# One more pair of every feed-forward way out by the seven-product scheme, the last pair's operands kept on chip, loads in a fixed order; FFN 2's pairs in another order with two more early products

## The chip, the cores and the metric

The kernel runs on one core of a Trainium2 chip. Its engines work side by side, each through its own instructions in order: TensorE (PE in the profile) multiplies, VectorE (DVE), ScalarE (ACT) and GpSimd (POOL) work on tiles, and SyncE (SP) issues nearly all transfers. An engine waits on semaphores that other engines or transfers raise. The metric is the device time of one execution in microseconds (us), lower is better. A difference below 0.2% (about 4 us) can't be told from no change here.

## The reference, cut to what matters

One layer on x of 1024 tokens by 1024 channels, in float32; D_FF is 2816:

```
x = x + 0.5 * swiglu_ffn(rms_norm(x, norm_ffn1), ffn1_w_in, ffn1_w_out)
x = x + token_mixer(rms_norm(x, norm_mix), w_in, w_out, ...)
x = x + 0.5 * swiglu_ffn(rms_norm(x, norm_ffn2), ffn2_w_in, ffn2_w_out)
return rms_norm(x, norm_final)

swiglu_ffn(x, w_in, w_out): gate, up = split(x @ w_in); return (silu(gate) * up) @ w_out
```

The change touches only the two feed-forward networks (FFN 1, FFN 2) and the last norm; the four token mixers between them stay.

## The kernel before, in words

**Precision.** Every operand of a product is split into a high and a low part in a reduced float32 (tiles `whi`/`wlo` for weights; the two halves of an `xs`, `xe` or `hx` tile for activations). ScalarE casts the high part, VectorE subtracts to get the low one, and `acc3` makes one product of three matmuls: weight-high with both parts, weight-low with the high one.

**Seven products.** The 2816 hidden channels are 22 tiles of 128, taken as 11 pairs p = 0 to 10. A two-by-two block product is done by seven products instead of eight (Strassen's scheme in Winograd's form), in the order ORDER7 = 1, 2, 5, 7, 6, 3, 4. `left` makes the weight sums (`wsum`) and operands for it; `seven` runs the products and adds results (ScalarE copies some out of PSUM, GpSimd adds the kept ones, VectorE adds the rest). In the way in, `pair` does gate and up of one pair so, 168 matmuls in all. For a few pairs products 1 and 2 (the corner) were done early, by `corner`: the first four (CORNERS) in the mixers and the next MORE at the start of FFN 2, before pair 0. Such a pair has 120 matmuls left.

**The way out.** The hidden values of a pair that goes out by seven products are added to seven combinations, split, and written to memory as seven tiles `hs` (`put_seven`, 512 KB each). `out_seven` reads them back: the nine pairs below STRASSEN = 9 go in blocks, first pair 0 alone, then four blocks of two pairs. A block has four quarters q of 256 output channels. A quarter loads its weights (`wraw`, 512 KB), makes operands, does seven products, and adds them onto the accumulators x (tiles `gr` and `gg`): ScalarE halves a product into a `tmp` or `hx` tile, VectorE adds onto x, GpSimd adds the rest (`plus`). The hidden values of pairs 9 and 10 are written plainly, loaded again, and multiplied by the ordinary way (96 matmuls a pair instead of 84) after the blocks. In FFN 2 `token_major` transposes x on TensorE ahead of that plain part, which works token tile by token tile: the first 512 output channels (c = 0) for eight token tiles tt, then the others (c = 1). Once a token tile has both, `final_sum` and `final_norm` make the last norm of it: GpSimd makes the factor `frs` in three small operations, VectorE scales both halves, SP and ScalarE send them out.

**Order.** The code is written in program order, and a scheduler then orders each engine's instructions by what is ready; where the code says `keep_in_program_order`, the order in the code stands. A tile name has a fixed number of buffers (bufs): a load into it waits until the buffer's last reader is done. SP takes its transfers in order, so what stands behind a waiting load waits as well.

Of the kernel before, what the change touches and what calls it, by code (L numbers as in the profile page):

```python
# [26 lines left out]
CORNERS, MORE, STRASSEN, URGENT = 4, 2, 9, 80  # L27
# [73 lines left out]
class Trunk:  # L101
# [26 lines left out]
    def wload(self, src, nk, c, splits=2):  # L128

        nc = self.nc  # L130
        raw = self.wp.tile([P, 1088], F32, name="wraw")
        rv = raw[:, :nk * c].rearrange("p (k c) -> p k c", c=c)
        for ap, off, n in src:
            nc.sync.dma_start(rv[:, :, off:off + (n or c)], ap)
        step = nk // splits
        res = []
        for s in range(splits):
            hi = self.wp.tile([P, 544], F32R, name="whi", bufs=4)
            lo = self.wp.tile([P, 544], F32R, name="wlo", bufs=4)
            sl = slice(s * step * c, (s + 1) * step * c)  # L140
            n = step * c
            nc.scalar.copy(hi[:, :n], raw[:, sl])  # L142
            nc.vector.tensor_tensor(lo[:, :n], raw[:, sl], hi[:, :n].bitcast(F32), op=ALU.subtract)  # L143
            for j in range(step):
                res.append((hi[:, j * c:(j + 1) * c], lo[:, j * c:(j + 1) * c]))
        return res
# [138 lines left out]
    def left(self, wk, raw, corner=False):  # L285
# [5 lines left out]
        def add(x, y, op):  # L291
            t = wk.tile([P, H], F32, name="wsum", bufs=3)
            nc.vector.tensor_tensor(t, x, y, op=op)
            return t

        def halves(a):
            hi = self.wp.tile([P, 544], F32R, name="whi", bufs=4)
            lo = self.wp.tile([P, 544], F32R, name="wlo", bufs=4)
            nc.scalar.copy(hi[:, :H], a)  # L299
            nc.vector.tensor_tensor(lo[:, :H], a, hi[:, :H].bitcast(F32), op=ALU.subtract)  # L300
            return [(hi[:, j * P:(j + 1) * P], lo[:, j * P:(j + 1) * P]) for j in range(4)]

        if not corner:
            yield halves(a11)
            yield halves(a12)
        s1 = add(a21, a22, ALU.add)
        yield halves(s1)
        s2 = add(s1, a11, ALU.subtract)
        yield halves(add(a11, a21, ALU.subtract))
        yield halves(s2)  # L310
        yield halves(add(a12, s2, ALU.subtract))
        yield halves(a22)
# [40 lines left out]
    def pair(self, wk, raws, right, p, p1=(None, None)):  # L353
# [9 lines left out]

        def up(i, h, ps, other):
# [3 lines left out]
            if p >= STRASSEN:  # L368
                self.put_h(u, 2 * p + i, h)

        def ups():
            if p1[0] is not None and p < STRASSEN:
# [3 lines left out]
            if p < STRASSEN:  # L376
                self.put_seven(wk, us, p)
# [3 lines left out]
    def put_seven(self, wk, us, p):  # L381
# [3 lines left out]
        def put(n, t):  # L385
            x = wk.tile([P, 2 * H], F32R, name="hx", bufs=3)
# [34 lines left out]
    def ffn1_in(self, wk, w_in):  # L421

        nc = self.nc
        self.xd, self.hd, self.hs, self.which = {}, {}, {}, 1
# [35 lines left out]
        for p in range(1, FT // 2):  # L460
            raws = [self.pair_weights(wk, w_in, p, o) for o in (0, DFF)]
            for t in self.pair(wk, raws, right, p):
# [17 lines left out]
    def ffn2_in(self, wk, w_in):  # L480

        nc = self.nc
        self.which, self.spare, self.turn, self.hs = 2, None, 0, {}
# [36 lines left out]
        for p in range(1, FT // 2):  # L520
            raws = [self.pair_weights(wk, w_in, p, o) for o in (0, DFF)]
            for t in self.pair(wk, raws, right, p, self.p1.get(p, (None, None))):
                for _ in t:
                    pass
# [27 lines left out]
    def out_seven(self, wk, w_out, slot, tmp):  # L552
# [4 lines left out]
        blocks = [(0, STRASSEN % 2)] if STRASSEN % 2 else []  # L557
        blocks += [(b, 2) for b in range(STRASSEN % 2, STRASSEN, 2)]

        def weights(b0, nb, q):  # L560

            raw = self.wp.tile([P, 1088], F32, name="wraw")[:, :nb * 512]
# [1208 lines left out]
```

## Time and profile before

| | us |
|---|---|
| three timed runs | 2102.67, 2103.93, 2104.75 (median 2103.93) |
| the profiled execution | 2101.29, of which 2099.5 is the span that the profile shows |
| TensorE busy | 1998.7 (95% of the span) |
| VectorE busy | 1491.5 (71%) |
| ScalarE busy | 966.2 (46%) |
| GpSimd busy | 417.3 (20%) |

TensorE works nearly all the time, so the time is made of its matmuls and of the stretches in which it waits. By the timeline FFN 1's way in runs to about 482 us and its way out to about 665 us, the mixers to about 1441 us, FFN 2's way in to about 1854 us and its way out to the end. In a row of the timeline the first number is the start, the second how long the group ran, and the brackets at its end tell how long the engine had been idle before it, and what it waited for.

### The profile page before, as it was taken

The page shows a single profiled execution, that of the slowest core. Times are in us where ns is not written, and L with a number is a line of the kernel's source. Part 1 is how long each engine was busy: PE and PEld are TensorE (multiplying, and loading weights), DVE is VectorE, ACT ScalarE, POOL GpSimd, SP SyncE. Part 2 cuts the span into 40 slices and gives each one's busy share as a digit, 9 for nine tenths or more (in the row PEclk, how much of TensorE's full clock was granted, in tenths as well). Part 3 has the DMA queues.
Part 4 walks back from the last instruction along what each step waited for, and adds up shares of the span by engine and source line. Part 5 has one row for each costly group of instructions (what it writes and reads, how often), then busy time and mean ns, then how long its engine had stood idle before and what let it go on. Part 6 is the DMA issues. An engine that isn't in the chain of part 4 may idle for free. (4 is left out here: it accounts for less than half of the span.)

```text
span 2099.5 us, 29339 instructions
## 1 busy us (share of the span) xinstructions
PE 1998.7 (95%) x10448; PEld 1603.6 (76%) x10448; DVE 1491.5 (71%) x2564; ACT 966.2 (46%) x1808; POOL 417.3 (20%) x430
## 2 busy tenths in 40 slices
PE   6999999998999999989999999899899999979998
PEld 4688888886887778777788787687677788868876
DVE  6967768656769556587665676667988877558784
ACT  6544444434434464443554534434544545334443
POOL 0100000004446502011020010100232200044461
PEclk9999999998999999999999999999999999989999
DMA  5444444448573453333452335544466545396632
GB/s 197 136 139 151 161 131 160 151 150 311 194 272 116 148 151 101 106 95 101 145 153 82 111 113 165 185 153 152 150 215 205 202 139 181 115 349 248 227 104 80
DMA packets 289139, 338.13 MB, mean 161 GB/s; under 512 B 27744, under 2 KB 216512, under 8 KB 288992
## 3 DMA queue, kind: packets, MB, share of 16 engines
q1 hardware_dynamic: 285888, 328.65, 47.2%
q0 software_dynamic: 1664, 4.95, 0.7%
q10 hardware_dynamic: 1440, 2.65, 0.3%
q8 instruction: 82, 1.34, 0.3%
q14 instruction: 65, 0.53, 0.1%
HBM read 225.83 MB, written 110.36 MB: 160 GB/s over the span
## 5 line engine op out<-in xcount | busy, mean ns | idle before, releaser
L86 PE MATMUL mm<-xs,whi 128*128 128x512 f32 x1664 | 546.4, 409 | 24.6 <-ACT whi L573 21.3
L86 PEld LDWEIGHTS mm<-xs,whi 128*128 128x128 f32 x1664 | 303.8, 191 | 97.5 <-ACT whi L573 23.0
L86 PE MATMUL mm<-xs,wlo 128*128 128x512 f32 x832 | 331.6, 399 | 2.8 <-DVE wlo L574 1.8
L86 PEld LDWEIGHTS mm<-xs,wlo 128*128 128x128 f32 x832 | 158.7, 191 | 43.1 <-DVE wlo L574 3.9
L86 PE MATMUL pq<-xs,whi 128*128 128x512 f32 x576 | 181.8, 397 | 3.6 <-ACT whi L299 3.6
L299 ACT CAST whi<-wsum 128x512 fp32r<-128x512 f32 x176 | 108.3, 620 | 160.4 <-PE pq L86 53.6
L142 ACT CAST whi<-wraw 128x512 fp32r<-128x512 f32 (+1 forms) x176 | 108.2, 620 | 155.2 <-PE mm L86 121.9
L143 DVE TENSOR_TENSOR wlo<-wraw,whi 128x512 fp32r<-128x512 f32 (+1 forms) x176 | 124.5, 714 | 64.9 <-ACT whi L142 41.6
L86 PE MATMUL px<-xs,whi 128*128 128x512 f32 x512 | 161.1, 396 | 0.0
L86 PE MATMUL pg<-xs,whi 128*128 128x512 f32 x496 | 157.5, 397 | 3.0 <-ACT xs L174 2.7
L300 DVE TENSOR_TENSOR wlo<-wsum,whi 128x512 fp32r<-128x512 f32 x176 | 119.3, 688 | 21.0 <-ACT whi L299 20.8
L86 PE MATMUL pq<-xe,whi 128*128 128x512 f32 x416 | 131.6, 398 | 0.8 <-DVE xe L175 0.8
L86 PEld LDWEIGHTS pq<-xs,whi 128*128 128x128 f32 x576 | 108.9, 190 | 29.7 <-ACT whi L299 5.2
L86 PE MATMUL pq<-xs,wlo 128*128 128x512 f32 x288 | 115.0, 399 | 5.7 <-DVE wlo L300 5.7
L339 POOL TENSOR_TENSOR tmp<-tmp 128x512 f32<-128x512 f32 x22 | 35.1, 1595 | 398.8 <-ACT tmp L329 398.8
L86 PEld LDWEIGHTS px<-xs,whi 128*128 128x128 f32 x512 | 96.9, 190 | 21.8 <-ACT whi L299 0.2
L86 PEld LDWEIGHTS pg<-xs,whi 128*128 128x128 f32 x496 | 93.9, 190 | 25.2 <-ACT xs L174 3.5
L300 DVE TENSOR_TENSOR wlo<-wraw,whi 128x512 fp32r<-128x512 f32 x64 | 44.0, 691 | 83.2 <-ACT whi L299 83.2
L339 POOL TENSOR_TENSOR gr<-gr 128x512 f32<-128x512 f32 x20 | 42.7, 2135 | 300.9 <-ACT gr L329 282.7
L86 PE MATMUL px<-xs,wlo 128*128 128x512 f32 x256 | 101.3, 396 | 0.1
L86 PE MATMUL pg<-xs,wlo 128*128 128x512 f32 x248 | 98.5, 397 | 0.0
L86 PE MATMUL px<-xe,whi 128*128 128x512 f32 x304 | 95.3, 394 | 0.3 <-ACT gr L329 0.3
(454 smaller groups left out, 4285.0 us busy)
## 6 DMA issues: line engine op xcount, KB each, us to landing
hs<-hx SPq DMA_DIRECT2D x126, 512.0 KB, 3.4
xs<-hs SPq DMA_DIRECT2D x94, 512.0 KB, 7.2
wraw<-in_ffn_w_in SPq DMA_DIRECT2D x56, 512.0 KB, 3.9
wraw<-in_w_in SPq DMA_DIRECT2D x52, 512.0 KB, 4.1
wrawb<-in_ffn_w_in SPq DMA_DIRECT2D x44, 512.0 KB, 4.6
wraw<-in_ffn_w_out SPq DMA_DIRECT2D x40, 512.0 KB, 3.6
xe<-hs SPq DMA_DIRECT2D x32, 512.0 KB, 7.1
wraw<-in_w_out SPq DMA_DIRECT2D x16, 512.0 KB, 4.1
```

Source lines behind the costliest of these rows:

```text
L86: return self._add(self.nc.tensor.matmul(out, lhsT=lhsT, rhs=rhs, **kw), n * 0.42e-3 if rhs.dtype == F32R else max(n * 1.68e-3, 0.04))
L142: nc.scalar.copy(hi[:, :n], raw[:, sl])
L143: nc.vector.tensor_tensor(lo[:, :n], raw[:, sl], hi[:, :n].bitcast(F32), op=ALU.subtract)
L299: nc.scalar.copy(hi[:, :H], a)
L300: nc.vector.tensor_tensor(lo[:, :H], a, hi[:, :H].bitcast(F32), op=ALU.subtract)
L339: nc.gpsimd.tensor_tensor(kept[5], kept[5], kept[7], op=ALU.add)
```

## The change

- Both ways out send ten pairs by seven products in five blocks of two, and one pair the plain way (`PLAIN`).
- FFN 1: the plain pair is p = 10. Its operands are split where they are made and stay in four `xs` tiles (`keep`), and it goes out first. Its weights, the x tiles and the first block's `hs` tiles are loaded in a fixed order. Then come the blocks (0,1), (2,3), (4,5), (6,7), (8,9). While a block runs, the next one's `hs` tiles are fetched in a fixed order too: two in each of the quarters 0 to 2, and the other eight in quarter 3 (`early` = 6).
- FFN 2: the plain pair is p = 0 and goes out last. The way in goes through the pairs in the order 0, 1, 8, 2, 3, 9, 4, 5, 6, 7, 10. The seven tiles of pair 10 stay on chip, those of pair 9 are loaded back during pair 10, and the block (9,10) goes out first, then (1,2), (3,4), (5,6), (7,8). MORE goes from 2 to 4: pairs 4 to 7 have their corner done before pair 0. Half of the transposes move into the last block.
- Weight operands: `whi` and `wlo` have two buffers of 1088 columns instead of four of 544, and a cast or subtraction makes the operands of two products at once.
- The last norm: for the first seven token tiles the second half is scaled by ScalarE and multiplied by the gain on GpSimd, not on VectorE.

```diff
-CORNERS, MORE, STRASSEN, URGENT = 4, 2, 9, 80
+CORNERS, MORE, URGENT = 4, 4, 80
+PLAIN = {1: FT // 2 - 1, 2: 0}
+ORDER2 = (0, 1, 8, 2, 3, 9, 4, 5, 6, 7, 10)
...
+    def wtiles(self):
+        return self.wp.tile([P, 1088], F32R, name="whi", bufs=2), self.wp.tile([P, 1088], F32R, name="wlo", bufs=2)
...
+        def operands(a, n):
+            hi, lo = self.wtiles()
+            nc.scalar.copy(hi[:, :n * H], a)
+            nc.vector.tensor_tensor(lo[:, :n * H], a, hi[:, :n * H].bitcast(F32), op=ALU.subtract)
...
+            if keep is not None:
+                keep[p, n] = self.split(t)
+                return
...
+        for p in ORDER2[1:]:
             raws = [self.pair_weights(wk, w_in, p, o) for o in (0, DFF)]
...
+            if last:
+                for n in self.ORDER7:
+                    t = self.xp.tile([P, 2 * H], F32R, name="xs", bufs=16)
+                    self.fetch_hs(t, p - 1, n)
...
+    def fetch_hs(self, t, p, n):
+        self.tc.keep_in_program_order(self.nc.sync.dma_start(t.bitcast(F32), self.hs[p, n]))
...
+        def fetch(b0, q):
             raw = self.wp.tile([P, 1088], F32, name="wraw")[:, :nb * 512]
+            self.tc.keep_in_program_order(nc.sync.dma_start(
+                raw.rearrange("p (f c) -> p f c", c=256), wo[:, 2 * b0:2 * b0 + 2 * nb, q * 256:(q + 1) * 256]))
+            return raw
...
+        for i, b0 in enumerate(blocks):
+            last = i == len(blocks) - 1
+            nhs, load = ({}, iter(())) if last else self.ahead(slot, (blocks[i + 1], blocks[i + 1] + 1))
+            done = 0
             for q in range(4):
+                if i == 0 and before is not None:
+                    before(q)
+                raw = fetch(b0, q)
+                while done < (early * (q + 1) // 3 if q < 3 else 99):
+                    done += 1
+                    if next(load, self) is self:
+                        done = 99
...
+            if i % 14 in (5, 12, 13):
+                return wk.tile([P, 2 * H], F32R, name="xe", bufs=4)
+            return self.xp.tile([P, 2 * H], F32R, name="xs", bufs=16)
...
+        self.out_seven(wk, w_out, slot, lambda: wk.tile([P, H], F32, name="tmp"), (0, 2, 4, 6, 8), hs, 6)
...
+        self.out_seven(wk, w_out, slot, tmp, (p0, 1, 3, 5, 7), hs, 12, load_acc, after)
...
+            if c == 0 or tt == 7:
+                self.tc.keep_in_program_order(
+                    nc.vector.scalar_tensor_tensor(a[c], a[c], r, g, op0=ALU.mult, op1=ALU.mult))
+            else:
+                nc.scalar.activation(a[c], a[c], AF.Identity, scale=r)
+                nc.gpsimd.tensor_tensor(a[c], a[c], g, op=ALU.mult)
```

Three places show how instructions move. The first is SP in FFN 1's way out, around the change from one block of two pairs to the next. `hs1_p_n` is product n's tile of pair p in FFN 1, and `wraw` are a quarter's weights. Before, at the change from the block (1,2) to (3,4):

```order
L563 DMA wraw_4600<-in_ffn1_w_out 128x4x256
L563 DMA wraw_4711<-in_ffn1_w_out 128x4x256
L597 DMA xs_4695<-hs1_3_6_1727 128x1024
L597 DMA xs_4697<-hs1_4_6_2064 128x1024
L597 DMA xe_4689<-hs1_4_5_2052 128x1024
L597 DMA xe_4691<-hs1_3_7_1721 128x1024
L597 DMA xs_4699<-hs1_3_3_1732 128x1024
L597 DMA xs_4701<-hs1_4_3_2069 128x1024
L597 DMA xs_4703<-hs1_3_4_1738 128x1024
L597 DMA xs_4705<-hs1_4_4_2075 128x1024
L563 DMA wraw_4794<-in_ffn1_w_out 128x4x256
```

`wraw_4600` is quarter 3 of the block (1,2), and `wraw_4711` quarter 0 of the block (3,4): it stands ahead of eight of that block's `hs` loads. After, at the change from the block (0,1) to (2,3):

```order
L594 DMA wraw_4209<-in_ffn1_w_out 128x4x256
L566 DMA xs_4211<-hs1_2_7_1300 128x1024
L566 DMA xs_4213<-hs1_3_7_1609 128x1024
L566 DMA xs_4215<-hs1_2_6_1306 128x1024
L566 DMA xs_4217<-hs1_3_6_1615 128x1024
L566 DMA xs_4219<-hs1_2_3_1311 128x1024
L566 DMA xs_4221<-hs1_3_3_1620 128x1024
L566 DMA xe_4223<-hs1_2_4_1317 128x1024
L566 DMA xe_4225<-hs1_3_4_1626 128x1024
L594 DMA wraw_4304<-in_ffn1_w_out 128x4x256
L566 DMA xs_4306<-hs1_4_1_1901 128x1024
```

`wraw_4209` is quarter 3 of the block (0,1), and `wraw_4304` quarter 0 of the block (2,3): it now stands behind all fourteen of its block's `hs` loads.

The second place is GpSimd at the end of the program, in the last norm. `frs` is a token tile's factor, `fss` the sums of squares it comes from, and `wrawb` holds the gain. Before:

```order
L778 TENSOR_TENSOR frs_18684<-fss_18503 128x1
L779 TENSOR_SCALAR frs_18684<-frs_18684 128x1
L780 TENSOR_TENSOR frs_18684<-frs_18684,mhalf_78 128x1
L778 TENSOR_TENSOR frs_18708<-fss_18520 128x1
L779 TENSOR_SCALAR frs_18708<-frs_18708 128x1
L780 TENSOR_TENSOR frs_18708<-frs_18708,mhalf_78 128x1
```

After:

```order
L823 TENSOR_TENSOR frs_17786<-fss_17634 128x1
L824 TENSOR_SCALAR frs_17786<-frs_17786 128x1
L825 TENSOR_TENSOR frs_17786<-frs_17786,mhalf_78 128x1
L833 TENSOR_TENSOR xe_17457<-xe_17457,wrawb_17560 128x512
L823 TENSOR_TENSOR frs_17805<-fss_17651 128x1
L824 TENSOR_SCALAR frs_17805<-frs_17805 128x1
L825 TENSOR_TENSOR frs_17805<-frs_17805,mhalf_78 128x1
L833 TENSOR_TENSOR xe_17477<-xe_17477,wrawb_17560 128x512
```

Between the factors of two token tiles GpSimd now multiplies half a token tile.

The third place is ScalarE where FFN 2's way in ends. L327 (L329 before) copies products out of PSUM, L573 (L605 after) casts weights of the way out, and L174 casts hidden values. Before:

```order
L329 COPY gr<-px 128x512
L573 CAST whi<-wraw 128x256
L329 COPY gr<-pq 128x512
L573 CAST whi<-wsum 128x256
L329 COPY gr<-mm 128x512
L573 CAST whi<-wsum 128x256
```

After:

```order
L327 COPY gr<-pq 128x512
L327 COPY gr<-mm 128x512
L174 CAST xs<-gr 128x512 x5
L605 CAST whi<-wraw 128x512
L605 CAST whi<-wraw 128x256
L174 CAST xs<-gr 128x512
```

The first cast for the way out now stands behind five casts of pair 10's hidden values.

More of the change, by code (lines that the diff above doesn't have):

```diff
@@ L362, in gated @@
             gate[i, h] = g
+        plain = p == PLAIN[self.which]
         def up(i, h, ps, other):
@@ L461, in ffn1_in @@
             raws = [self.pair_weights(wk, w_in, p, o) for o in (0, DFF)]
-            for t in self.pair(wk, raws, right, p):
+            for t in self.pair(wk, raws, right, p, keep=self.kept if p == PLAIN[1] else None):
                 for _ in t:
@@ L550, in keep_p1, with ahead, steps, out_seven @@
         self.p1[p].append(d)
-    def out_seven(self, wk, w_out, slot, tmp):
+    def fetch_hs(self, t, p, n):
+        self.tc.keep_in_program_order(self.nc.sync.dma_start(t.bitcast(F32), self.hs[p, n]))
+    def ahead(self, slot, pairs):
+        hs = {}
+        def steps():
+            for n in self.ORDER7:
+                for r, p in enumerate(pairs):
+                    t = slot()
+                    self.fetch_hs(t, p, n)
+                    hs[n, r] = (t[:, 0:H], t[:, H:2 * H])
+                    yield
+        return hs, steps()
+    def out_seven(self, wk, w_out, slot, tmp, blocks, hs, early, before=None, after=None):
         nc = self.nc
@@ new lines, in ffn1_out, with wraw @@
+        f0 = 2 * PLAIN[1]
+        hs, load = self.ahead(slot, (0, 1))
+        def wraw(n):
+            raw = self.wp.tile([P, 1088], F32, name="wraw")[:, :512]
+            tc.keep_in_program_order(nc.sync.dma_start(raw.rearrange("p (f c) -> p f c", c=256),
+                                                       wo[:, f0:f0 + 2, n * P:(n + 2) * P]))
+            return raw
+        for n in range(0, KT, 2):
+            raw = wraw(n)
+            for h in range(2):
+                self.x[n, h]
+                tc.keep_in_program_order(nc.sync.dma_start(self.x["t", n // 2, h], self.xd[n // 2, h]))
+            for _ in range(4):
+                next(load, None)
+            hi, lo = self.wtiles()
+            nc.scalar.copy(hi[:, :512], raw)
+            nc.vector.tensor_tensor(lo[:, :512], raw, hi[:, :512].bitcast(F32), op=ALU.subtract)
@@ L725, in ffn2_out, with after @@
+        def after(m):
+            i = self.ORDER7.index(m)
+            token_major(i, 0)
+            if i == 6:
+                token_major(7, 0)
+        f0 = 2 * PLAIN[2]
+        p0 = FT // 2 - 2
+        hs = {(n, r): self.kept[p0 + r, n] for n in self.ORDER7 for r in range(2)}
+        self.out_seven(wk, w_out, slot, tmp, (p0, 1, 3, 5, 7), hs, 12, load_acc, after)
+        gf = wk.tile([P, D], F32, name="wrawb", bufs=2)
         nc.scalar.dma_start(gf, self.A["norm_final"].broadcast_to([P, D]))
```

248 lines of the change are left out of this document (105 added, 143 removed).

## The prediction

> **What bounds the kernel now.** I read the page first (who is busy, how long transfers take), then the table of stretches, then TensorE's timeline for the rows with idle time. The page:
>
> ```profile
> span 2099.5 us, 29339 instructions
> PE 1998.7 (95%) x10448; PEld 1603.6 (76%) x10448; DVE 1491.5 (71%) x2564; ACT 966.2 (46%) x1808; POOL 417.3 (20%) x430
> xs<-hs SPq DMA_DIRECT2D x94, 512.0 KB, 7.2
> wraw<-in_ffn_w_out SPq DMA_DIRECT2D x40, 512.0 KB, 3.6
> ```
>
> TensorE is idle for some 100 us of 2099.5. The stretches tell where (the columns are the length, then each engine's busy time, the granted clock, the share of time the transfer engines worked, and GB/s):
>
> ```profile
> 480.00:510.00 30.00, 19.95 (x68) 14.97 (x67) 17.02 (x38) 12.17 (x25) 11.82 (x9) 0.77 0.95 366
> 510.00:630.00 120.00, 120.00 (x520) 97.38 (x519) 87.16 (x141) 47.88 (x86) 57.78 (x38) 1.00 0.62 225
> 1441.00:1510.00 69.00, 58.54 (x242) 45.53 (x243) 61.44 (x99) 32.38 (x57) 10.09 (x6) 0.95 0.40 126
> 1510.00:1640.00 130.00, 124.82 (x527) 99.35 (x526) 113.37 (x175) 59.47 (x107) 36.01 (x18) 0.99 0.66 222
> 1640.00:1845.00 205.00, 205.00 (x888) 166.64 (x887) 145.00 (x234) 93.16 (x166) 17.81 (x12) 1.00 0.47 160
> 1845.00:1880.00 35.00, 23.01 (x87) 17.97 (x86) 19.46 (x41) 14.39 (x30) 15.67 (x12) 0.83 1.01 375
> ```
>
> The steady parts (510 to 630, 1640 to 1845) have no gap. The gaps lie where a way in becomes a way out (480 to 510, 1845 to 1880: transfers at full rate, TensorE waiting), and where FFN 2 begins (1441 to 1510: VectorE is busy 61.44 of 69). TensorE's rows there:
>
> ```profile
> 483.27 0.73 PE L86 MATMUL mm<-xs,whi 128*128 128x512 f32 x2 [0.79 <-ACT whi L573]
> 484.99 0.50 PE L86 MATMUL mm<-xs,wlo 128*128 128x512 f32 x1 [0.75 <-DVE wlo L574]
> 504.35 1.22 PE L86 MATMUL mm<-xs,whi 128*128 128x512 f32 x2 [8.51 <-ACT whi L573]
> 508.36 1.05 PE L86 MATMUL pg<-xs,whi 128*128 128x512 f32 x2
> 509.50 0.62 PE L86 MATMUL px<-xe,whi 128*128 128x512 f32 x2
> 1469.22 0.73 PE L86 MATMUL pq<-xs,whi 128*128 128x512 f32 x2 [1.96 <-ACT whi L299]
> 1470.38 0.50 PE L86 MATMUL pq<-xs,wlo 128*128 128x512 f32 x1 [0.43 <-DVE wlo L300]
> 1473.97 0.73 PE L86 MATMUL pq<-xs,whi 128*128 128x512 f32 x2 [1.02 <-ACT whi L299]
> 1489.28 0.97 PE L86 MATMUL pq<-xe,whi 128*128 128x512 f32 x3 [0.84 <-DVE xe L175]
> 1495.29 0.80 PE L86 MATMUL pq<-xe,wlo 128*128 128x512 f32 x1 [5.04 <-DVE wlo L300]
> 1503.08 0.72 PE L86 MATMUL pq<-xs,whi 128*128 128x512 f32 x2 [0.59 <-ACT whi L299]
> 1860.31 1.22 PE L86 MATMUL mm<-xs,whi 128*128 128x512 f32 x2 [5.96 <-ACT whi L573]
> 1878.19 1.22 PE L86 MATMUL mm<-xs,whi 128*128 128x512 f32 x2 [6.04 <-ACT whi L573]
> 2037.92 0.52 PE L735 MATMUL px<-ident,gr 128*128 128x128 f32 x3 [2.61 <-DVE gg L615]
> ```
>
> After a long wait two matmuls take 1.05 us (508.36), later 0.62 (509.50), and the stretch shows a granted clock of 0.77: some 9 matmuls at 0.43 us instead of 0.23 cost about 1.8 us on top of the wait.
>
> **What puts the first weights late.** The wait of 8.51 us is the model for what I expect after the change. SP issued two weight tiles at 492.82, behind fourteen `hs` loads, and ScalarE could cast the first at 503.68:
>
> ```profile
> 492.82 1.89 SPq L563 DMA_DIRECT2D wraw<-in_ffn_w_out  x2
> 503.68 0.62 ACT L573 CAST whi<-wraw 128x512 fp32r<-128x512 f32 x1 [8.53 <-DMA wraw<-in_ffn_w_out]
> DMA to landing us min/median/max: 3.3/7.3/9.9
> ```
>
> The last row is for the way out's weight loads in the whole blocks of FFN 1: there they land in 3.3 to 9.9 us, and nobody waits, since they are issued early.
>
> **The change, part by part.**
>
> 1. *Matmuls.* One pair per way out takes 84 instead of 96, so 24 fewer. Twelve took 2.79 us (the first row of the last fence), so 0.2325 each: **-5.6**.
>
> 2. *FFN 1, way in to way out.* The plain pair's operands are on chip and its weights are a small load: the waits of 0.79, 0.75 and 8.51 us go, with two clock losses (some 3 us). In their place TensorE waits for pair 10's last hidden value (an add, a product, a cast and a subtraction of 0.6 to 0.7 us each, of which some lies under the last product), about 2 us. Then the plain part runs 96 matmuls, 22 us, while x, fourteen `hs` tiles and the weights of the first block come in, about 12 MB (x 4.2, the tiles 7.3, the weights the rest); at the 366 GB/s of 480 to 510 that is 32 us, of which some 6 fit before the end of the way in. The first block's weight is behind them: a wait of 0 to 5 us, I take 2.5. Gain 13 less 4.5: **-9** (-13 to -4).
>
> 3. *FFN 1, the four changes of block.* The order shows quarter 0's weight of the next block behind all fourteen of its loads. The last of them goes into an `xe` buffer, of which there are four with three used per block, so it waits for product 4 of pair r = 0 in the last quarter: its reader ends three matmuls (0.7 us) before the block does. SP then issues that load, and the weight behind it about 0.2 us before the block ends. No other engine queues behind SP, but all of TensorE's work does. If the weight lands 3.3 us later (the shortest row), the cast of 0.62 follows and TensorE waits 3.7 us. If it lands as at 492.82, in 10.6, the wait is 11. Eight loads go out from 9 us before the end, at 1.4 us each (512 KB at 375 GB/s), so about two are still under way: I take a landing of 4.7 us, a wait of 5 and a clock loss of 1.5, 6.5 in all. Before, the same weight went out ahead of eight loads, and 510 to 630 shows 120.00 of 120 us busy. Four times 6.5: **+26** (+15 to +45).
>
> The Trainium skill, "DMA: Bandwidth & Descriptors", in Anatomy of one DMA, gives about 2.0 us plus the bytes at 436 GB/s for a transfer, and says that a semaphore wait happens on the issuing sequencer before dispatch. By its figures the weight would be there 3.2 us after its issue, the wait 3.6 us, and the four changes, at an estimate, +20 with the clock loss, a sum lower by 6. This case's trace shows 3.3 at best and a median of 7.3, so I stay with the rows.
>
> 4. *FFN 1's end.* The accumulators now end in a block, whose last adds are two in a row on GpSimd at about 1.5 us each, where a plain part ended with one VectorE operation: **+2.5** (0 to 4).
>
> 5. *FFN 2's start.* Two more corners are 96 matmuls, 22 us of TensorE work moved here (no more in all), while VectorE makes the first operands. The waits from 1469 to 1503 (1.96, 5.04 and four of 0.4 to 1.0, together 9.9) can go, and a clock loss with them; VectorE's share of 61.44 in 69 leaves room only because the corners need little of it: **-9** (-11 to -3).
>
> 6. *Corner pairs.* In them VectorE is late:
>
> ```profile
> 1548.94 0.50 PE L86 MATMUL pq<-xs,wlo 128*128 128x512 f32 x1 [0.61 <-DVE wlo L300]
> 1579.68 0.50 PE L86 MATMUL pq<-xs,wlo 128*128 128x512 f32 x1 [2.27 <-DVE wlo L300]
> 1610.02 0.50 PE L86 MATMUL pq<-xs,wlo 128*128 128x512 f32 x1 [0.72 <-DVE wlo L300]
> ```
>
> From 1548.94 to 1610.02 are two pairs, 30.5 us each, where 120 matmuls need 27.9: 2.6 us lost a pair. Two more such pairs cost up to +5; the wider operations (one cast and one subtraction for two products) and the new order may save as much over eight pairs, or cost. I take **+2.5** (-6 to +12). In the other pairs the two-buffer operands leave VectorE and ScalarE one product, 2.8 us, to make the next pair of operands; a cast and a subtraction of twice the width take, at twice 0.62 and 0.69, at most 2.6. I cost that at nothing: the cover is the last product, and the third matmul, the first to need the low part, comes 0.5 us later still.
>
> 7. *FFN 2, way in to way out.* The waits of 5.96 and 6.04 us with two clock losses, 15.6 us, were for weights behind `hs` loads. Pairs 9 and 10 are on chip now, so the weights come early; but the first cast for the way out stands behind five casts of hidden values, which wait for VectorE's chain of adds and subtractions after the last product. Ten operations of 0.6 to 0.7 us, partly side by side, make about 8 us of waiting, and one clock loss: 9.6. **-6** (-12 to -2).
>
> 8. *FFN 2's end.* Here the matmul count misleads. The end before:
>
> ```profile
> 2066.79 2.79 PE pg L86 x12
> 2069.58 1.63 PE mm L86 x7
> 2094.99 0.75 DVE xe L782
> 2085.21 0.48 POOL L778 TENSOR_TENSOR frs<-fss 128x1 f32<-128x1 f32 x1 [1.40 <-ACT hx L772]
> 2085.78 0.19 POOL L779 TENSOR_SCALAR frs<-frs 128x1 f32<-128x1 f32 x1
> 2086.05 0.55 POOL L780 TENSOR_TENSOR frs<-frs,mhalf 128x1 f32<-128x1 f32 x1
> L618 POOL TENSOR_TENSOR gr<-gr,hx 128x512 f32<-128x512 f32 x35 | 52.6, 1503 | 89.0 <-DVE gr L615 66.1 <-ACT whi L573 16.4 <-ACT hx L611 5.2
> L300 DVE TENSOR_TENSOR wlo<-wsum,whi 128x512 fp32r<-128x512 f32 x176 | 119.3, 688 | 21.0 <-ACT whi L299 20.8
> ```
>
> The second half of the output (c = 1) begins at 2069.58, takes TensorE 2.79 us a token tile, and the span ends 29.9 us later. GpSimd needs 1.4 us a token tile for the factor (2085.21 to 2086.60). With one pair plain, TensorE needs 1.4 us a tile, but GpSimd has the factor and half a tile to multiply: 1.4 plus 1.5 (L618's mean) is 2.9 us. So the half is bound by GpSimd: 5 us until its first product starts, 7 times 2.9, one more factor, the last tile's VectorE work and the store (4.5 us from 2094.99 to the end) make about 28 us. The 48 matmuls taken from this half, 11.2 us, bring only about 2.5. So step 1 is too good by **+8.7** (+6 to +11).
>
> 9. *The wait at 2037.92.* 2.61 us and part of a clock loss: the transposes of the first half now lie in the last block, the rest wait for fewer adds: **-2.5** (-4 to 0).
>
> Sum: -5.6 - 9 + 26 + 2.5 - 9 + 2.5 - 6 + 8.7 - 2.5 = +7.6. The profiled execution was 2101.3 us (1.8 outside the span), 2.6 below the median of 2103.9, so I expect 2108.9 where that one stood, and 2111.5 against the median.
>
> **The rivals.**
>
> *The changes of block cost nothing or little; faster.* Then the sum is -18, 2085.5. Place: SP at the end of FFN 1's blocks. For it speaks that 510 to 630 leaves 38% of the transfer time free, and that a load with nothing ahead can land in 3.3; against it, that the order leaves SP no way past the load that waits. It decides at 4.6 us a change: below that the kernel gets faster. At the shortest landing and no clock loss, 3.7 us, it would be 2100.3, the edge of "same".
>
> The Trainium skill, "TensorE: Matmul & The Clock Gate", Part 1, puts the clock at half after an idle window of about 3.4 us; by it a wait under that would lose no clock. The row at 2037.92 (2.61 us) can't settle it, since its stretch holds short transposes, and no row shows a wait of 3 to 5 us inside a block.
>
> *The operands come late in every pair; slower still.* Two buffers in place of four take away the lead of the next weights. If VectorE's subtraction comes 0.3 us late at some 44 changes of operand in the ways in, that is +13, 2124.5. For it: 113.37 of 130 us of VectorE in the corner pairs. Against it: 145.00 of 205 in the others, where the sum of step 6 leaves 0.7 us.
>
> *The gains are smaller.* Steps 2, 5 and 7 at their weak ends give +15 more, 2126; all three would have to fail, so it gets little.
>
> **How the numbers follow.** The forecast, with each change of block at 5 to 8 us and the gains near their values, spans 2104 to 2120: 0.45. The changes of block at 3 us or less: 0.28. Between, at 3 to 5: 0.12. Late operands or small gains: 0.15. The range is 2086 (the first rival) to 2127. A measurement tells 0.2% (4.2 us) from no change: faster than 2099.7, 0.29; within, 0.17; slower, 0.54.
>
> **What would show it.** Right: four waits of 4 to 8 us on `whi` from L605 in FFN 1's way out, each about 39 us apart plus the wait, released by the weight's transfer, with SP idle before the `xe` load on a matmul; no wait of 8 us at FFN 1's way out's beginning; idle VectorE and a busy GpSimd in the last 25 us, with TensorE done some 15 us before the end; one wait instead of two at FFN 2's way out. Wrong: FFN 1's way out without gaps (step 3 falls), rows "pq <- DVE wlo" of half a microsecond in every pair (the two buffers), or waits of several microseconds at the block changes of FFN 2, which I cost at nothing because its `xe` has twelve buffers and the next weight stands behind loads that wait only for the last quarter's first two products.

## The result, and the profile after

The changed kernel takes 2161.47 us (median of four runs, 2150.15 to 2169.98); the kernel before, run beside it, 2104.34 (2102.67 to 2113.05). The ratio is 1.026, with a 95% interval of 1.0204 to 1.0315. The forecast was 2111.5 and its range ended at 2127: the sign was right, and the size missed by 50 us.

The page of the changed kernel, the same lines as before:

```profile
span 2160.8 us, 28709 instructions
PE 1998.7 (92%) x10424; PEld 1608.1 (74%) x10424; DVE 1505.0 (70%) x2449; ACT 947.3 (44%) x1691; POOL 414.5 (19%) x441
xs<-hs SPq DMA_DIRECT2D x98, 512.0 KB, 7.4
wraw<-in_ffn_w_out SPq DMA_DIRECT2D x42, 512.0 KB, 6.5
```

TensorE is busy for the same 1998.7 us, so the 61 us of span are idle time. (That 24 fewer matmuls take the same time hides a faster pace and slower stretches that cancel, both below.) Weights of the way out need 6.5 us to land, where they needed 3.6. TensorE's waits, summed by what ended them (us in total, times, longest):

```profile
PE mm L88 <- ACT whi L605: 35.9, 6, 7.4
PE px L88 <- DVE wlo L294: 16.7, 13, 2.3
PE mm L88 <- DVE wlo L142: 12.7, 5, 5.3
PE mm L88 <- DVE wlo L294: 9.2, 12, 3.4
```

L605 casts weights for the ways out, L294 makes low parts of the way in's weights, L142 those of the mixers' first weights. The stretches (columns as before) put them in their places: FFN 1's way in to way out, its five blocks, the mixers' beginning, FFN 2's start, its way in, its way in to way out, and the second half of the output:

```profile
460.00:505.00 45.00, 39.32 (x160) 30.16 (x159) 24.95 (x40) 9.28 (x16) 2.54 (x2) 0.96 0.93 348
505.00:735.00 230.00, 198.10 (x821) 158.13 (x819) 155.67 (x237) 85.48 (x158) 92.86 (x66) 0.94 0.49 178
735.00:770.00 35.00, 17.68 (x59) 14.20 (x60) 22.49 (x33) 13.03 (x24) 34.53 (x34) 0.61 0.25 78
1488.00:1545.00 57.00, 53.92 (x234) 44.03 (x234) 49.82 (x80) 30.19 (x51) 1.17 (x2) 0.97 0.55 165
1545.00:1860.00 315.00, 295.62 (x1264) 236.95 (x1263) 248.49 (x345) 132.61 (x200) 58.94 (x36) 0.99 0.54 179
1895.00:1945.00 50.00, 39.50 (x160) 30.72 (x158) 28.70 (x55) 20.13 (x37) 13.83 (x10) 0.90 0.63 235
2130.60:2160.80 30.20, 11.05 (x49) 8.82 (x47) 18.34 (x18) 10.86 (x26) 17.84 (x31) 0.73 0.37 139
```

The way out of FFN 1, without a gap before from 510 to 630, now has TensorE busy 198 of 230 us. At the mixers' beginning TensorE works half the time, and GpSimd 34.53 of 35 us. FFN 2's start has become nearly full. Three places in detail.

**A change of block in FFN 1's way out** (SP's queue, then the cast and the first matmul):

```profile
529.95 4.40 SPq L566 DMA_DIRECT2D xs<-hs  x6
534.40 4.03 SPq L566 DMA_DIRECT2D xe<-hs  x2
538.52 0.39 SPq L594 DMA_DIRECT2D wraw<-in_ffn_w_out  x1
544.91 0.92 ACT L605 CAST whi<-wraw 128x512 fp32r<-128x512 f32 x2 [8.23 <-DMA wraw<-in_ffn_w_out]
545.58 1.22 PE L88 MATMUL mm<-xs,whi 128*128 128x512 f32 x2 [6.82 <-ACT whi L605]
```

Two `xe` loads hold SP for 4.03 us, the weight goes out at 538.52, 0.24 us before the block's last matmul ends (545.58 less 6.82), and lands some 6.3 us later. Four changes wait 6.82, 7.43, 7.06 and 7.01 us.

**The mixers' beginning:**

```profile
739.51 0.80 PE L88 MATMUL mm<-xs,wlo 128*128 128x512 f32 x1 [5.29 <-DVE wlo L142]
747.62 0.74 PE L88 MATMUL mm<-xs,whi 128*128 128x512 f32 x2 [3.47 <-ACT whi L141]
752.50 0.79 PE L88 MATMUL mm<-xs,wlo 128*128 128x512 f32 x1 [4.14 <-DVE wlo L142]
758.49 1.65 PE L88 MATMUL px<-ones,o 128*128 128x1 f32 x7 [5.21 <-POOL o L209]
743.48 16.18 POOL L209 TENSOR_TENSOR o<-o,tmp 128x512 f32<-128x512 f32 x11
727.98 1.77 DVE L178 SCALAR_TENSOR_TENSOR xs<-gr,vec,xs 128x512 fp32r<-128x512 f32 x1
729.68 0.68 DVE L648 SCALAR_TENSOR_TENSOR gr<-pg,gr 128x512 f32<-128x512 f32 x1
```

L209 adds the squares for the mixers' norm, on GpSimd, and eleven such additions are left when FFN 1 ends. L178 makes that norm's operands on VectorE.

**A corner pair of FFN 2's way in**, in the chain that ended last:

```profile
1645.51 1.14 DVE wlo L294
1646.69 2.56 PE px L88 x10
1649.26 2.51 PE pq L88 x11
1651.83 0.63 ACT whi L293
1652.49 0.70 DVE wlo L294
1653.20 5.57 DMA wrawb<-in_ffn_w_in
1658.80 0.04 DVE wsum L302
```

TensorE waits for a low part (1.38 us at 1646.69). The cast of the pair's last operands, at 1651.83, comes only behind a product on TensorE (`pq`) that frees their buffer. The pair's last low part, at 1652.49, is the last reader of a `wrawb` buffer, so the load into that buffer starts only then, and the next operands wait for the load.

### The profile page after: what moved, and what is told of

Read it like the earlier page. It is cut to its first block, busy times and chain, and to the rows that moved or that the text cites. A ratio compares the mean times of both kernels' runs of the same rounds, so it can differ in the third digit from the quotient of the medians.

```text
span 2160.8 us, 28709 instructions
## 1 busy us (share of the span) xinstructions
PE 1998.7 (92%) x10424; PEld 1608.1 (74%) x10424; DVE 1505.0 (70%) x2449; ACT 947.3 (44%) x1691; POOL 414.5 (19%) x441
## 5 line engine op out<-in xcount | busy, mean ns | idle before, releaser
L88 PE MATMUL px<-xs,whi 128*128 128x512 f32 x568 | 179.1, 396 | 1.4 <-ACT tmp L644 0.8
L141 ACT CAST whi<-wraw 128x512 fp32r<-128x512 f32 (+2 forms) x170 | 99.0, 624 | 129.2 <-PE mm L88 75.2
L88 PE MATMUL pq<-xe,whi 128*128 128x512 f32 x464 | 144.3, 392 | 0.3 <-ACT tmp L644 0.2
L293 ACT CAST whi<-wsum 128x1024 fp32r<-128x1024 f32 x88 | 92.4, 1050 | 104.2 <-PE pg L88 37.8
L88 PE MATMUL px<-xs,wlo 128*128 128x512 f32 x284 | 113.5, 400 | 16.7 <-DVE wlo L294 16.7
L142 DVE TENSOR_TENSOR wlo<-wraw,whi 128x512 fp32r<-128x512 f32 (+2 forms) x170 | 116.1, 703 | 6.9 <-ACT whi L141 6.5
L294 DVE TENSOR_TENSOR wlo<-wsum,whi 128x1024 fp32r<-128x1024 f32 x88 | 108.0, 1227 | 4.4 <-ACT whi L293 4.4
L337 POOL TENSOR_TENSOR tmp<-tmp 128x512 f32<-128x512 f32 x22 | 31.2, 1418 | 400.1 <-ACT tmp L327 400.1
L88 PEld LDWEIGHTS pq<-xe,whi 128*128 128x128 f32 x464 | 87.7, 189 | 19.6 <-ACT tmp L644 1.1
L88 PE MATMUL pq<-xe,wlo 128*128 128x512 f32 x232 | 90.9, 392 | 2.0 <-DVE wlo L294 2.0
L651 POOL TENSOR_TENSOR gr<-gr,tmp 128x512 f32<-128x512 f32 x41 | 59.8, 1460 | 155.9 <-DVE gr L648 129.1
```

The lines of the kernel that those rows point to most:

```text
L88: return self._add(self.nc.tensor.matmul(out, lhsT=lhsT, rhs=rhs, **kw), n * 0.42e-3 if rhs.dtype == F32R else max(n * 1.68e-3, 0.04))
L141: nc.scalar.copy(hi[:, sl], raw[:, sl])
L142: nc.vector.tensor_tensor(lo[:, sl], raw[:, sl], hi[:, sl].bitcast(F32), op=ALU.subtract)
L293: nc.scalar.copy(hi[:, :n * H], a)
L294: nc.vector.tensor_tensor(lo[:, :n * H], a, hi[:, :n * H].bitcast(F32), op=ALU.subtract)
L337: nc.gpsimd.tensor_tensor(kept[5], kept[5], kept[7], op=ALU.add)
```

## The experiments

Every kernel was timed beside the kernel before; its ratio to that is what counts, since runs of one kernel spread by up to 1.3% (27.5 us in e2 below). The prediction took 0.2% for the least difference that a measurement can tell; that was too little.

**e1_before**: the kernel before once more, unchanged.

> The kernel before, unchanged, profiled once more beside the others. In the profile before a matmul of 128x512 follows the one ahead after 0.2314 us wherever TensorE doesn't wait; in the changed kernel after 0.2269 us, in the untouched mixers too. If that belongs to the kernels, this run shows 0.2314 and about 2101 to 2105 us. If it belongs to the chip or to the moment, this run may show 0.227 and some 2065 us, and the change then cost some 20 to 40 us more than the two profiles say when one is set against the other.

2104.63 us, its span 2102.9 us: the profile before is a typical one.

**e2_weight_ahead**: the changed kernel, in FFN 1 with the next block's first weight ahead of the last quarter's loads.

```diff
-                raw = fetch(b0, q)
+                raw = nraw if q == 0 and i > 0 and self.which == 1 else fetch(b0, q)
+                if q == 3 and not last and self.which == 1:
+                    nraw = fetch(blocks[i + 1], 0)
```

> The changed kernel, but in FFN 1's way out quarter 0's weight of the next block is issued ahead of the last quarter's eight loads, as it was before the change. If these weights are late only because they stand behind a load that waits for the block's last product (my step 3), the four waits of 6.8 to 7.4 us on the first cast go, 28 us, and with them four clock losses of about 1.8: some 35 us faster, about 2126. Rival: the transfers themselves are the bound there; then the wait moves to the tiles loaded behind the weight, and the gain is under 15 us.

2135.12 us (2124.61 to 2152.11), ratio 1.0133 (1.0074 to 1.0191): 26 us less than the changed kernel. The sum of waits on that cast:

```profile
PE mm L88 <- ACT whi L605: 7.6, 4, 6.4
PE mm L88 <- DVE wlo L606: 15.8, 15, 2.9
```

The four waits of 7 us are gone; what is left is mainly the one at FFN 2's way out. But the low parts of the same weights (L606) are now waited for 15.8 us, 7.1 in the changed kernel. So the order on SP cost 26 us net. That this is to the microsecond what step 3 had is luck: each of the two ratios is known to 0.6%, some 12 us.

**e3_four_buffers**: the changed kernel with operands made product by product again, in four buffers of 544 columns.

```diff
-        return self.wp.tile([P, 1088], F32R, name="whi", bufs=2), self.wp.tile([P, 1088], F32R, name="wlo", bufs=2)
+        return self.wp.tile([P, 544], F32R, name="whi", bufs=4), self.wp.tile([P, 544], F32R, name="wlo", bufs=4)
...
-            yield from operands(ra[:, 0:2 * H], 2)
+            yield halves(a11)
+            yield halves(a12)
```

> The changed kernel, but weight operands are made as before the change, one product (in the way out two) at a time into four buffers of 544 columns. If the waits on the low part of the weights in the ways in (28 us on L294 in all, 1.2 to 2.0 us in each half of a corner pair) come from the two wide buffers, they fall to the level before (13 us or less, 0.7 to 2.3 a pair), and it is 12 to 20 us faster. Rival: they come from having two more corner pairs and from the weights' transfers; then it stays within 5 us.

2149.17 us (2141.25 to 2156.8), ratio 1.0179 (1.0132 to 1.0225): 12 us less than the changed kernel, though the two intervals overlap. In the profiles TensorE's waits fall by 24 us, from 141.7 to 117.4 in all. The other half was taken back by the matmuls themselves. In the stretch from 300 to 360 us, inside FFN 1's way in, of the kernel before and of the changed one:

```profile
300.00:360.00 60.00, 60.00 (x261) 48.80 (x260) 42.86 (x68) 27.43 (x49) 4.01 (x3) 1.00 0.38 125
300.00:360.00 60.00, 59.70 (x264) 49.12 (x263) 43.56 (x62) 27.95 (x41) 4.02 (x3) 1.00 0.40 137
```

TensorE does 261 matmuls there before and 264 after, though it waits 0.3 us in between, and 261 again in e3. Nobody waits in the stretch before; the matmul's own pace differs, 0.2314 us to 0.2269 from start to start over the way in. What it follows is the subject of the next four runs.

**e5_before_576**: the kernel before with operand buffers of 576 columns instead of 544 (the additional columns stay empty), and the scratch memory for transfers as in the changed kernel, which makes room for them.

```diff
-            hi = self.wp.tile([P, 544], F32R, name="whi", bufs=4)
+            hi = self.wp.tile([P, 576], F32R, name="whi", bufs=4)
...
-    nc = _bacc.Bacc("TRN2", target_bir_lowering=False, num_devices=1)
+    nc = _bacc.Bacc("TRN2", target_bir_lowering=False, num_devices=1, dynamic_dma_scratch_size=8192)
```

> The kernel before with its four weight operand buffers 576 columns wide instead of 544 (and a smaller scratch area for transfers, as in the changed kernel, to make room). Nothing else changes; the extra columns are not used. So far the pace of matmuls follows the operand tiles: 0.2314 us with four buffers of 544 columns (the kernel before, and the changed kernel with these), 0.2269 with two of 1088. With 544 columns every other buffer starts 128 bytes off a multiple of 256 from the first one, with 1088 or 576 all start alike. If the place of the buffers sets the pace, this run shows 0.227 and is some 25 to 40 us faster than before, 2065 to 2080. Rival: the pace follows from how many products one operand tile serves; then it stays at 0.2314 and 2100 to 2107.

2088.0 us (2086.85 to 2089.92), ratio 0.9892 (0.9857 to 0.9926): faster by 1.1% for empty columns.

```profile
300.00:360.00 60.00, 60.00 (x266) 49.70 (x265) 45.93 (x75) 29.87 (x53) 4.02 (x3) 1.00 0.44 149
```

The pace is the expected one, 0.2267 us; the time isn't, 2088 where 2065 to 2080 was said. In the mixers the matmuls of 512 columns gain less (0.2313 to 0.2303 us), and TensorE's waits grow by 5 us.

**e14_before_scratch**: only the scratch memory of e5.

```diff
-    nc = _bacc.Bacc("TRN2", target_bir_lowering=False, num_devices=1)
+    nc = _bacc.Bacc("TRN2", target_bir_lowering=False, num_devices=1, dynamic_dma_scratch_size=8192)
```

> The kernel before with only the scratch memory for transfers set as in the kernel after, and its four operand buffers of 544 columns. The kernel before with buffers of 576 columns had both and took 2088.0 us. Theory that the place of the operand buffers sets the matmul's pace: no change, ratio 0.998 to 1.002, and 261 matmuls in the stretch from 300 to 360 us. Rival, the scratch memory did it: ratio 0.989, and 266 matmuls there.

2106.02 us, ratio 0.9985 (0.9964 to 1.0007), and

```profile
300.00:360.00 60.00, 60.00 (x261) 48.80 (x260) 42.68 (x69) 26.63 (x48) 4.01 (x3) 1.00 0.40 130
```

So it is the buffers, not the scratch memory.

**e9_1120**: the changed kernel with its two buffers 1120 columns wide instead of 1088.

```diff
-        return self.wp.tile([P, 1088], F32R, name="whi", bufs=2), self.wp.tile([P, 1088], F32R, name="wlo", bufs=2)
+        return self.wp.tile([P, 1120], F32R, name="whi", bufs=2), self.wp.tile([P, 1120], F32R, name="wlo", bufs=2)
```

> The changed kernel with its two weight operand buffers 1120 columns wide instead of 1088, the extra columns unused. The second buffer of each kind then starts 128 bytes off a multiple of 256 from the first, as with 544 columns. If the place of the buffers sets the pace of matmuls, it goes from 0.2269 to 0.231 us, with the wide operations unchanged. Rival: the pace belongs to wide operands and stays at 0.227.

2170.18 us in one run, and a pace of 0.2300 us, between the two. Its products of twelve matmuls take about 2.73 and 2.79 to 2.80 us, mostly two and two in turn, as each of its wide buffers serves two products. In the kernel before they take 2.76 and 2.80 in turn, one by one, as each narrow buffer serves one. In e5 all take 2.72. So the pace goes with the buffer that a product's weights lie in, and not with its width: in e9 two buffers of one width differ. Buffers of 576 and 1088 columns of four bytes are multiples of 256 bytes; 544 and 1120 columns are half of 256 over, so that every second buffer starts at another place within 256 bytes. All four are multiples of 128 bytes, and 576 and 1088 columns aren't multiples of 512, so the place within 256 bytes is what tells the fast from the slow here. Why it should matter, the runs don't show.

**e15_after_576**: the changed kernel with four buffers of 576 columns, e3 at the good pace.

```diff
-            hi = self.wp.tile([P, 544], F32R, name="whi", bufs=4)
+            hi = self.wp.tile([P, 576], F32R, name="whi", bufs=4)
```

(against e3)

> The kernel after with four operand buffers of 576 columns in place of two of 1088, and no weight ahead. If the late weight at the changes of block (26 us by its own experiment) and the late operands (28 us between two profiles with the weight ahead) add up, this takes 2161 less 28 to 36, 2125 to 2133, a ratio near 1.009, and the four waits of 7 us stay. Rival, the one hides behind the other (late operands would have come to rest behind the long waits): 2115 or less, or 2145 or more.

2130.49 us (2126.97 to 2132.03), ratio 1.0101 (1.0075 to 1.0126): 31 us less than the changed kernel. The late operands cost that much (in the ways out and the mixers too, whose operands come through the same buffers), and the late weights are untouched:

```profile
PE mm L88 <- ACT whi L612: 37.3, 9, 7.6
```

**e6_ahead_576**: e15 with the weight ahead as in e2.

> The changed kernel with the next block's first weight issued ahead in FFN 1, and with weight operands made product by product in four buffers, here of 576 columns. The two alone gave 26 us and 12 us. If they add up, and the pace of matmuls follows the place of the buffers (0.227), it is 2161 less 38 less some 30, about 2093. Rival: the pace stays at 0.2314; then about 2123.

2100.89 us (2088.61 to 2109.34), ratio 0.9947 (0.9922 to 0.9972). That is 30 us less than e15, and 34 less than e2: the two losses add up. But it has the pace that alone gave e5 1.1%, so against e5 it still loses 13 us.

**e10_ffn1_before**: e15 with FFN 1's way out as it was before (nine pairs, two of them written and loaded for the plain part), FFN 2 as changed.

```diff
-        plain = p == PLAIN[self.which]
+        plain = p >= STRASSEN if self.which == 1 else p == PLAIN[2]
...
-            for t in self.pair(wk, raws, right, p, keep=self.kept if p == PLAIN[1] else None):
+            for t in self.pair(wk, raws, right, p, keep=None):
...
+    def out_seven_1(self, wk, w_out, slot, tmp):
```

> FFN 1's way out as before the change (nine pairs in blocks of one and two, two pairs plain at the end), FFN 2 as in the changed kernel, operands product by product in four buffers of 576 columns. Against the kernel before with the same buffers (2088.0 us) only FFN 2 is changed. Between the second norm and the end the profile of the changed kernel with such buffers is 6 us shorter than that of the kernel before with them: so I expect 2080 to 2084. Rival: FFN 2's part gains nothing in the time, since its end is bound by the last norm; then 2086 to 2092.

2082.8 us (2073.48 to 2085.42), ratio 0.9878 (0.9834 to 0.9921). FFN 2's changes leave e5's ratio of 0.9892 where it was, within the intervals; FFN 1's new way out, even with its weights early, costs some 14 us (against e12, below) to 18 us (against e6). Where, the next three tell.

**e7_plain_last**: e2 with FFN 1's plain pair last, written and loaded again.

```diff
+        self.out_seven(wk, w_out, slot, lambda: wk.tile([P, H], F32, name="tmp"), (0, 2, 4, 6, 8), hs, 6, load_acc,
+                       raw0=raw0)
+        def h_tile(f, h):
+            t = wk.tile([P, H], F32, name="tmp")
+            nc.sync.dma_start(t, self.hd[f, h])
+            return self.split(t)
...
-        self.out_seven(wk, w_out, slot, lambda: wk.tile([P, H], F32, name="tmp"), (0, 2, 4, 6, 8), hs, 6)
```

> The changed kernel with the first weight ahead, and FFN 1's plain pair done last again, its operands written and loaded back as before the change. To be set against the run with the weight ahead alone (2135 us). If the waits where the mixers begin (18 us, and clock losses of some 5) come from GpSimd, which must add both the last block's products and the squares for the norm, they fall to the 4 us of before; the wait of 8 to 10 us at the beginning of FFN 1's way out comes back in place of 4.6. Net about 12 us faster, 2123. Rival: those waits come from elsewhere and stay; then it is 5 us slower, 2140.

2147.57 us, ratio 1.0155 (1.0107 to 1.0203), no better than e2. The waits at the way out's beginning are back, and the mixers' beginning has one wait instead of four:

```profile
504.25 1.22 PE L88 MATMUL mm<-xs,whi 128*128 128x512 f32 x2 [8.93 <-ACT whi L605]
736.57 0.79 PE L88 MATMUL mm<-xs,wlo 128*128 128x512 f32 x1 [11.14 <-DVE wlo L142]
```

One plain pair is 22 us of matmuls, and sixteen norm operands of 0.74 to 1.78 us each stand on VectorE ahead of the mixers' first low parts. Before, the 44 us of two plain pairs had covered them.

**e12_squares_vectore**: e6 with the squares added on VectorE.

```diff
-            nc.gpsimd.tensor_tensor(self.sq[h], self.sq[h], t, op=ALU.add)
+            (nc.vector if self.which == 1 else nc.gpsimd).tensor_tensor(self.sq[h], self.sq[h], t, op=ALU.add)
```

> The changed kernel with the first weight ahead and four buffers of 576 columns (2100.9 us), and with the squares for the mixers' norm added up on VectorE instead of GpSimd. If the waits at the mixers' beginning (18 us there) come from GpSimd's chain of squares, which ends last, and from VectorE running at half its pace beside it (1.75 us for what takes 0.74 alone), they shrink by 6 us or more, 2094. Rival: VectorE has no room, and the waits stay or grow.

2096.93 us, ratio 0.9954 (0.9935 to 0.9973), no difference from e6. The four waits became three, 4.17, 4.13 and 6.34 us: VectorE's last five norm operands were quick again (0.74 to 0.75 us), but its queue was longer by the additions.

**e13_no_squares**: e6 without those additions on any engine, and without the squares that ScalarE makes for them. It leaves out all but the first square of each half, so its output is not the layer's.

```diff
+            if self.which == 1:
+                return
             t = wk.tile([P, H], F32, name="tmp")
```

> The kernel after with the weight ahead and four operand buffers of 576 columns (2100.89 us, ratio 0.9947), and in FFN 1's part the squares for the first two norms are left out but for the first channel tile, with their additions on GpSimd: the output is not the reference's. It asks what makes the mixers' beginning wait (5.25, 5.55, 1.99 and 6.43 us, 19.2 in all). Theory that GpSimd's sixteen additions hold it, by ending last and by slowing VectorE beside them: the waits fall to 6 us or less together, and the time lies 14 to 20 us lower, some 2083 or a ratio of 0.986. Rival, the order on VectorE (sixteen norm operands and the last sums ahead of the first low parts of the mixers' weights): waits of 10 us or more stay, and the time falls by 6 us or less, to a ratio of 0.992 or more. The program's beginning may lose up to 3 us of waiting in either case.

2085.02 us (2080.65 to 2087.49), ratio 0.9885 (0.9862 to 0.9908): 13 us less than e6 by the ratios, 16 by the medians. Of the mixers' beginning these waits are left:

```profile
703.76 0.79 PE L88 MATMUL mm<-xs,wlo 128*128 128x512 f32 x1 [4.15 <-DVE wlo L145]
708.40 0.50 PE L88 MATMUL mm<-xs,wlo 128*128 128x512 f32 x1 [0.15 <-DVE wlo L145]
713.76 2.68 PE L88 MATMUL px<-ident,rstok 128*128 128x128 f32 x9 [0.99 <-POOL rstok L231]
```

5.3 us of 19.2. The same lines make the first norm at the program's beginning, but no time was gained there: in the first 120 us the profile has 394 matmuls done, 405 in e6. So most of the loss hangs on the squares and their additions; e12 shows that the additions aren't to be had for nothing on VectorE either, and the rest (4.15 us) is a wait for a low part behind VectorE's norm operands.

**e8_two_corners**: the changed kernel with two early pairs at FFN 2's start instead of four.

```diff
-CORNERS, MORE, URGENT = 4, 4, 80
+CORNERS, MORE, URGENT = 4, 2, 80
```

> The changed kernel with MORE = 2, so two early corners fewer, as before the change. If the two extra corners save the waits at the beginning of FFN 2 (9.9 us before, my step 5) and cost about 2.7 us of waiting a pair later (1.4 to 2.0 in each half), it is some 4 to 6 us slower without them. Rival: two more early corners cost more than they save, since each of the eight pairs now waits on VectorE in both halves; then it is 3 us or more faster without them.

2160.53 us (2156.03 to 2162.38), ratio 1.0231 (1.0199 to 1.0262): no difference. The waits at the start are back,

```profile
1528.48 0.90 PE L88 MATMUL mm<-xe,whi 128*128 128x512 f32 x2 [4.28 <-ACT whi L293]
1537.02 0.50 PE L88 MATMUL mm<-xe,wlo 128*128 128x512 f32 x1 [3.07 <-DVE wlo L294]
```

and the waits in the pairs fall from 19.3 us to 10.0 in all. What the early products gain at the start (step 5) they lose in the pairs (step 6), at least with two buffers.

**e4_norm_vectore**: the changed kernel with the last norm wholly on VectorE, as before.

```diff
-            if c == 0 or tt == 7:
+            if True:
```

> The changed kernel, but the last norm scales both halves on VectorE, as before the change. If the end is bound by GpSimd (my step 8: factor and half a tile, 2.7 to 3.1 us a token tile, TensorE done 19 us before the end), VectorE needs 0.7 for the sum and 1.4 for the two halves, 2.1 us a tile, and the end comes 6 to 9 us sooner. Rival: VectorE at 2.1 us a tile and the wait of ScalarE behind the stores leave the end where it is, within 2 us.

2162.34 us (2151.04 to 2173.28), ratio 1.0253 (1.0203 to 1.0304): no difference in time. In its profile the second half takes 24.48 us where the changed kernel takes 30.20:

```profile
2134.22:2158.70 24.48, 11.05 (x49) 8.82 (x47) 16.99 (x25) 6.53 (x19) 11.23 (x24) 0.79 0.45 172
```

5.7 us can't be seen in runs that spread over 20 us. **e11_ffn1_before_norm** is e10 with the same edit:

> The same with the last norm on VectorE as before the change. In the profiles the stretch from the first product of the second half to the end was 30.2 us with GpSimd and 24.5 us with VectorE: 5 to 6 us faster than the run beside it, about 2076. Rival: no difference, as in the times of the changed kernel (2162 against 2161).

2076.78 us (2074.07 to 2081.04), ratio 0.9864 (0.9819 to 0.9909). It beats both kernels: 1.4% faster than before, 3.9% faster than the changed one (2076.78 to 2161.47). Against e10 the intervals overlap.

## Why the prediction was wrong

By the profiles, TensorE's idle time in each place, with an estimate in brackets of what the matmuls behind a wait took beyond the steady pace:

| step | forecast | before | after | found |
|---|---|---|---|---|
| 2, FFN 1 way in to out | -9 | 10.1 (2.3) | 5.6 (3.0) | -4 |
| 3, changes of block | +26 | 0 | 28.3 (9) | +37; e2: 26 |
| 4, mixers' beginning | +2.5 | 4.2 (1.4) | 18.1 (4.4) | +17; e13: 13 to 16 |
| 5, FFN 2's start | -9 | 11.0 (3.7) | 3.1 (2.4) | -9 |
| 6, FFN 2's pairs | +2.5 | 5.1 (4.1) | 19.3 (11.3) | +21 |
| 6, FFN 1's pairs | 0 | 0 (1.6) | 3.6 (3.7) | +6 |
| 7, FFN 2 way in to out | -6 | 12.0 (4.2) | 10.5 (4.0) | -2 |
| 1 and 8, matmuls, the last half | +3.1 | 29.9 | 30.2 | +6 |
| 9, wait before the last half | -2.5 | 2.6 | 2.0 | -1 |
| the matmul's pace | 0 | 0.2314 | 0.2269 | -17 to -25 (e5) |

The +6 is 24 matmuls less (-5.6), the 48 that left the last half (11.2 us) without making it shorter, and the 0.3 that it grew by. Step 6 is split by network. The last column sums to between +46 and +54, against a span longer by 61.

**Step 3 was right**, the mechanism to a tenth of a microsecond (SP released 0.24 us before the block's end, where 0.2 was said). The landing was 6.3 us instead of 4.7, the waits 7 instead of 5, and so the profile has +37. That e2 gave back just 26 fits the 8.7 us more of waiting for low parts there.

**Step 6 failed, and is the largest miss.** It had two terms. The corner pairs stood at +2.5, between -6 and +12, for a VectorE that is late. The other pairs were put at nothing: "I cost that at nothing: the cover is the last product". Both terms missed: of the 19.3 us of waits in FFN 2's pairs 14.9 lie in the corner pairs (5.1 before) and 4.4 in the others, and FFN 1's pairs, which have no corner, add 3.6. The sum took 2.6 us of work for the next operands and 2.8 us of cover as if the work started at once. But those operands need a buffer, so they start late; they are the last readers of a weight's buffer, so the next load starts late as well, and lands 5.57 us on (1653.20). The late operand repeats with every half of a corner pair; rows "DVE wlo" in FFN 2's pairs were named as a sign that would make the prediction wrong. It was one of the rivals, at 44 changes by 0.3 us (+13), with a chance of 0.15 that it shared with the small gains. e15 put it at 31 us: not 44 waits of 0.3 us but some 25 of 0.2 to 3.4, and slow matmuls behind some of the longer ones, which the rival had left out:

```profile
1792.51 0.66 PE L88 MATMUL px<-xs,wlo 128*128 128x512 f32 x1 [2.02 <-DVE wlo L294]
1792.96 1.05 PE L88 MATMUL px<-xs,whi 128*128 128x512 f32 x2
```

Two matmuls take 1.05 us after 2.02 us of waiting. The Trainium skill, "TensorE: Matmul & The Clock Gate", Part 1, which the prediction had weighed, has the clock at half after an idle window of about 3.4 us. That a wait under this would lose no clock, as the prediction worked out from it, this row contradicts, and the measurement decides.

**Step 4 failed.** It counted GpSimd's last two additions in a row, 1.5 us each. It didn't ask what else depended on the accumulators: sixteen squares, their additions and sixteen norm operands had run under 44 us of plain matmuls, and lost that cover. The trace of before had the answer, at L178 and L209, which run there from 675 to 717 us with pauses, under the plain part (FFN 1's way out ends with it, near 713 us; at 665, given as its end ahead of the prediction, only its blocks do):

```profile
675.29 0.75 DVE L178 SCALAR_TENSOR_TENSOR xs<-gr,vec,xs 128x512 fp32r<-128x512 f32 x1 [0.16 <-ACT xs L177]
679.60 3.46 POOL L209 TENSOR_TENSOR o<-o,tmp 128x512 f32<-128x512 f32 x2 [10.47 <-ACT tmp L208]
714.74 1.48 POOL L209 TENSOR_TENSOR o<-o,tmp 128x512 f32<-128x512 f32 x1 [0.86 <-ACT tmp L208]
```

Packed together, GpSimd and VectorE slow each other there: L178 takes 1.77 us beside GpSimd's additions, 0.75 at 675.29, while L648, which reads one operand from PSUM, stays at 0.68. L209's additions take about 1.7 us while VectorE works and 1.26 once it idles, from 753.5 us on. The Trainium skill, "SBUF — State Buffer", SBUF: two separate sides, has VectorE and GpSimd share a port pair that one instruction holds whole, where the VectorE operation has two inputs in SBUF: the rows agree, in that L178 is slowed and L648 is not.

**Steps 2 and 7 were too hopeful.** Two waits on weights stay in the plain part (1.85 and 2.71 us at 483.58 and 492.02), and FFN 2's way out begins with one wait of 6.44 us, one of 0.61 and three of 1.15 where 8 us in all were forecast. **Steps 1, 5 and 9** came out about as said. **Step 8** had the bound right and the size too small: the terms it lists (5, 7 times 2.9, 1.4 and 4.5) add to 31.2 us and not to about 28, and the half took 30.2. e4 shows that GpSimd's part in the norm made the end longer, by 5.7 us in the profile.

**The gain that nobody priced** was the pace. The prediction took 0.2325 us a matmul from before for granted. Without that gain the miss would have been about 70 us.

What stays open: why the pace depends on the buffers' place; how much of the mixers' beginning an order of VectorE's queue that puts the mixers' low parts first would bring (not tried); and some 10 us between the table's sum and the span, less than runs of one kernel differ by (3.4 of them are waits on weights in FFN 2's blocks from 1945 to 2090 us, which no step has).

## What to carry to other kernels

When buffers are merged into fewer and wider ones, the last reader of each decides when the next load starts: follow that chain (buffer, operand, load, next operand) once around before calling it covered. When a stage is moved from the end to the beginning, list everything that ran under it on the other engines, not only the waits at its two edges. And a load that everybody waits for goes ahead of those that wait for a buffer.

## What the runs showed of the hardware

The matmul's pace changes by 2% with the place of its weight operands in memory: 0.2314 us with buffers of 544 columns, 0.2267 with 576 and 0.2269 with 1088, 0.2300 with 1120, all over FFN 1's way in. The Trainium skill, "TensorE: Matmul & The Clock Gate", Part 1, gives 215.7 ns for 512 columns at the full clock; no run here kept that pace.

The length of a single wait didn't decide whether TensorE's clock fell. In the changed kernel it fell after waits of 2.02 us (1792.51), 2.31 (1536.73) and 2.71 (492.02), with six to eight matmuls some 0.43 us apart behind each, and not after 1.85 (483.58). But in e15 it fell after 1.84 us (1818.24) and not after 2.70 (485.50), and in e8 not after 3.07 (1537.02).
